# Filling behind the exact chain in priority, gates moved in front, memory's keys and values moved beside the delta rule

## The chip, the cores and the metric

One core of one Trainium2 chip runs the whole program in one launch. The metric is the device time of one execution in microseconds. Times come from repeated runs; the profile is of one execution of its own.

## The reference, cut to what matters

A model of three blocks on 512 tokens of width 1024. The change lies in the mixer of the first block alone:

```
mod = silu(c) @ ada_w + ada_b                      # six vectors of 1024
h = rms(x) * (1 + sc1) + sh1                       # the normed tokens
q_a, kv_a, gate_a, qkv_b, beta_b, a_b, z_b, merge = split(h @ w_in)
y_a = nsa(q_a, kv_a, gate_a)                       # sparse attention, 8 heads, 3 branches
y_b = gated_deltanet(conv(qkv_b), beta_b, a_b, z_b)  # delta rule, 8 heads, chunks of 64
#     decay: g = -exp(a_log) * softplus(a_b + dt_bias), cumulated
#     output: rms(o) * silu(z_b)
y = sigmoid(merge_0) * (y_a @ w_br_a) + sigmoid(merge_1) * (y_b @ w_br_b)
x = x + g1 * (y @ w_out)
```

Two later layers attend to a memory of 256 rows. Its keys and values, `rms(mem) @ x_wkv` for each of the two layers, depend on nothing else, so the kernel may compute them anywhere before.

## The kernel before, in words

A float32 product is done as three products of rounded parts: each operand is split in a high and a low part (`whi`, `wlo`; `ha`, `hl` for the normed tokens), and `mm3` adds high x high, high x low and low x high in PSUM. `gemm_fm` loads a weight block of 128 x 1024 (`wraw`, on SP's queue), splits it on ACT and then on DVE or POOL in turns, and multiplies: 24 products of 512 columns for the tokens, 24 of 256 for memory.

The exact chain (`exact_rstd`, `exact_mod`, `exact_decay`) follows the reference's order of additions to the bit: the norm, 32 paths for the modulation (tiles `xa`, `xd`, `xdc`, `xtc`, `xw`), 64 units for the decay's raw values (`aa`, `ad`, `at` and `adg` of ones and weights, `ahh`), then `decay_sums`, an exact softplus and cumulated sums of small operations. A unit goes PE, ACT, POOL, PE, ACT, then a scan on DVE, in two PSUM banks "x". Its result, the cumulated decay, is what the delta rule starts with.

`front` is the filling: memory's keys and values (`xkv`, two layers), `small1`, the convolutions for the delta rule (`dn_convs`), and sparse attention (`nsa`: compression, head part, body). `among` runs the chain as main and the filling as a generator; each DVE operation of the chain calls `spend`, which adds to a debt and advances the filling until its yields have paid it. So the order of the program interleaves both. A scheduler with a model of times then orders each engine's instructions: at each moment the ready instruction with the lowest priority number goes first, and the number counts up with the order of the program. It also gives tiles their bytes; a tile waits for the tile that had its bytes or its PSUM bank.

After the front the PSUM banks are divided anew and the delta rule runs: `dn_setup`, then `dn` with preparation, heads (two at a time, by turns with the next preparation) and two recurrences. `by_turns` advances `aside` once a round: 16 merge gates (`gates1`), each followed by two steps of `ada`. The output gates `dn_z` stand beside the last heads. Then `merge1` reads the gates back from memory.

Of the kernel before, what the change touches and what calls it, by code (L numbers as in the profile page):

```python
# [267 lines left out]
class Net:  # L268
    def __init__(self, ctx, tc, I, O):
        self.ctx, self.tc, self.nc, self.I, self.O = ctx, tc, tc.nc, I, O  # L270
        nc = self.nc
# [16 lines left out]
        self.gated = self.DR.tile([24, 128, S], F32, name="gated")  # L288
        self.dnd = self.DR.tile([12, 128, S], F32, name="dnd")
        self.mod = self.G.tile([128, 48], F32, name="mod")  # L290
# [41 lines left out]
    def among(self, other, ratio, main):  # L332
        self.other, self.ratio, self.debt = other, ratio, 0.0
        main()
        self.other = None
        for _ in other:
            pass

    def spend(self, out, more=0.0):
        if self.other is not None:  # L340
            self.debt += more or self.ratio * (0.2 + math.prod(out.shape[1:]) / 960)
            other, self.other = self.other, None
            while other is not None and self.debt > 0:
                c = next(other, None)
                if c is None:
                    other = None
                else:
                    self.debt -= c
            self.other = other

# [952 lines left out]
    def gates1(self, T):  # L1303

        for i in range(16):
            p = self.gemm_fm(self.I["w1_fm"][25 + i], self.ha, self.hl)
            self.nc.sync.dma_start(self.gated[i], self.sigmoid(T, p, [128, S], "mg"))
            yield

# [79 lines left out]
    def aside(self, A):  # L1389

        gates, ada = self.gates1(A), self.ada(A)
        for _ in range(16):
            next(gates)
            yield
            for _ in range(2):
                next(ada)
                yield
        for _ in ada:
            pass

    def dn(self, T, W):

        self.dT, self.dW = T, W
        self.pairs = [None] * 4
        turns = self.by_turns
        turns(self.dn_prep(0))
        turns(self.dn_head(0, 0), self.dn_head(0, 1), self.dn_prep(1))
        turns(self.dn_head(1, 0), self.dn_head(1, 1), self.dn_prep(2))
        turns(self.dn_head(2, 0), self.dn_head(2, 1), self.dn_recur(0))
        turns(self.dn_prep(3), self.dn_z(0))  # L1410
        turns(self.dn_head(3, 0), self.dn_head(3, 1), self.dn_gate(0))
        turns(self.dn_recur(1), self.dn_z(1))
        turns(self.dn_gate(1))

    def dn_convs(self, W):

        for pr in range(4):
            for c in (0, 4, 8):
                o = W.tile([128, S], F32, name="draw", bufs=2)
                self.conv_silu(W, o, 9 + c + pr, c + pr)  # L1420
                yield 4
                if c < 8:
                    sq = W.tile([128, S], F32, name="rsq", tag="rsq", bufs=1)
# [5 lines left out]
                self.nc.sync.dma_start(self.dnd[c + pr], o)  # L1429
                yield 2  # L1430

    def dn_prep(self, pr):
# [42 lines left out]
        P.update(qd=qd, kd=kd, kb=kb, kw=kw, vb=vb, at=T.tile([128, 2, 4, 128], F32, name="at", bufs=3),  # L1475
                 wt=T.tile([128, S], F32, name="wt", bufs=3), u=T.tile([128, 4, 128], F32, name="u", bufs=3))
        yield

    def dn_head(self, pr, par):
# [5 lines left out]
        def b4(p):  # L1485
            return p.rearrange("p (b i) -> p b i", b=4)
# [20 lines left out]
        for b in range(4):  # L1507
            c = slice(b * 128, (b + 1) * 128)
            self.mm(p[:, c], k[R, c], q[R, c])
        self.tt(P["at"][:, par], b4(p), mg, OP.mult)  # L1510
        yield
# [47 lines left out]
    def dn_recur(self, hf):  # L1559
# [6 lines left out]
        for c in range(8):  # L1566
# [25 lines left out]
            for hh in range(2):  # L1592
                H = slice(64 * hh, 64 * hh + 64)
                for pp in range(2):
                    self.mm(po[H, pp * 64:pp * 64 + 64], st[H, pp, :], P[pp]["qd"][H, cols])
                    self.mm(px[H, pp * 64:pp * 64 + 64], vn[R, pp, H], P[pp]["at"][R, hh, b, 64 * par:64 * par + 64])
            self.act(o[:, :, cols], po.rearrange("p (a d) -> p a d", a=2))
# [3 lines left out]

    def dn_z(self, hf):

        W = self.dW
        self.zs = []
        for pp in range(2):
            pz = self.gemm_fm(self.I["w1_fm"][21 + 2 * hf + pp], self.ha, self.hl)
            z = W.tile([128, S], F32, name="zg%d" % pp, tag=("kw", "vb")[pp], bufs=2)
            self.act(z, pz)
            s = self.sigmoid(W, z, [128, S], "cs")  # L1610
            self.tt(z, z, s, OP.mult)
            self.zs.append(z)
            yield

    def dn_gate(self, hf):
        W, o = self.dW, self.do
        for pp in range(2):
            self.rms64(W, o[:, pp, :], o[:, pp, :], self.pv("dng"), "do")
            self.tt(self.yb[:, 2 * hf + pp, :], o[:, pp, :], self.zs[pp], OP.mult)
            yield  # L1620
# [43 lines left out]
    def front(self, M):  # L1664

        for l in range(2):
            with self.pool("xf") as T:
                yield from self.xkv(T, l)
        self.small1(M)
        yield 5  # L1670
        with self.pool("dnC") as T:
            yield from self.dn_convs(T)
        with self.pool("nsaT") as T:
            yield from self.nsa(T)

    def block1_mixer(self, ctx):
        pool = self.pool
        with self.weights(2) as self.W, pool("Ya") as A, pool("sm") as M:
            self.ya = A.tile([128, 4, S], F32, name="ya")
            with ExitStack() as B:  # L1680
                with pool("X", side="right") as X:
                    with self.banks({"x": 2, "g": 3, "t": 2, "o": 1}, {"s": "g"}) as self.PS, pool("XR", side="right") as XR:
                        def main():
                            self.exact_rstd(XR)
                            self.fast_mod()
                            self.adaln1()
                            self.ratio = 0.7
                            self.exact(X)
# [400 lines left out]
    def xkv(self, T, l):  # L2089

        nc, I = self.nc, self.I
        m = T.tile([128, KT, 256], F32, name="mem")
        nc.sync.dma_start(m, I["memT"])
        r = self.rstd_x(T, m, 256)
        mh = T.tile([128, KT, 256], F32R, name="memh")
        ml = T.tile([128, KT, 256], F32R, name="meml")
        for k in range(KT):
            g = self.pv("g_mem", 8 * l + k)
            self.act(mh[:, k, :], m[:, k, :], AF.Copy, scale=g)
            self.stt(ml[:, k, :], m[:, k, :], g, mh[:, k, :].bitcast(F32), OP.mult, OP.subtract)  # L2100
        rt = T.tile([128, 2], F32, name="memr")
# [10 lines left out]
        for n in range(4):  # L2112
            pp = self.ps("g")
            for c in range(2):
                hi, lo = self.wslab(I["x_wv%d" % l][n * 2 + c])
                for kk in range(4):
                    k = 4 * c + kk
                    for b in range(2):
                        tk = slice(b * 128, b * 128 + 128)
                        self.mm3(pp[:, b * 256:(b + 1) * 256], mh[:, k, tk], ml[:, k, tk], hi[:, kk, :], lo[:, kk, :],  # L2120
                                 k == 0 and b == 0, k == 7 and b == 1)
            o = T.tile([128, 2, 256], F32, name="mvo", bufs=2)
            for b in range(2):
# [622 lines left out]
```

## Time and profile before

| | us |
|---|---|
| median of 3 runs | 4422.09 (4418.08 to 4423.69) |
| the profiled execution | 4420.88 |
| its span, first to last instruction | 4419.1 |
| PE busy in it | 4036.6 (91%) |
| weight loads (PEld) | 3236.0 (73%) |
| DVE, ACT, POOL busy | 2728.1, 2114.6, 1692.5 |

Busy time of an engine is the time in which at least one of its instructions runs, idle time the rest. PE is TensorE, PEld its weight loads, which overlap its products. The granted clock is TensorE's, as a share of full speed.

### The profile page before, as it was taken

The page shows a single profiled execution, that of the slowest core. Times are in us where ns is not written, and L with a number is a line of the kernel's source. Part 1 is how long each engine was busy: PE and PEld are TensorE (multiplying, and loading weights), DVE is VectorE, ACT ScalarE, POOL GpSimd, SP SyncE. Part 2 cuts the span into 40 slices and gives each one's busy share as a digit, 9 for nine tenths or more (in the row PEclk, how much of TensorE's full clock was granted, in tenths as well). Part 3 has the DMA queues.
Part 4 walks back from the last instruction along what each step waited for, and adds up shares of the span by engine and source line. Part 5 has one row for each costly group of instructions (what it writes and reads, how often), then busy time and mean ns, then how long its engine had stood idle before and what let it go on. Part 6 is the DMA issues. An engine that isn't in the chain of part 4 may idle for free. (4 is left out here: it accounts for less than half of the span.)

```text
span 4419.1 us, 55886 instructions
## 1 busy us (share of the span) xinstructions
PE 4036.6 (91%) x20436; PEld 3236.0 (73%) x20436; DVE 2728.1 (62%) x4770; ACT 2114.6 (48%) x3424; POOL 1692.5 (38%) x1144
## 2 busy tenths in 40 slices
PE   6999799869987989799899999999999899999998
PEld 4887676658866767678676777888777677777886
DVE  6657777677655778576566655332587475665542
ACT  4565668733332768433365544442344365444432
POOL 3342676523222353233254422332344264423431
PEclk8999899979978999899999999999999899999999
DMA  4432210034215889312131332223212122422232
GB/s 154 161 123 70 91 39 8 8 130 146 82 63 186 322 315 376 117 59 70 54 109 66 112 125 71 96 91 98 73 58 75 60 86 79 134 96 81 96 92 80
DMA packets 179605, 480.55 MB, mean 109 GB/s; under 512 B 17576, under 2 KB 28904, under 8 KB 178944
## 3 DMA queue, kind: packets, MB, share of 16 engines
q1 hardware_dynamic: 172512, 452.79, 30.0%
q0 software_dynamic: 6816, 24.15, 1.6%
q8 instruction: 163, 2.67, 0.2%
q14 instruction: 114, 0.93, 0.1%
HBM read 433.31 MB, written 41.44 MB: 107 GB/s over the span
## 5 line engine op out<-in xcount | busy, mean ns | idle before, releaser
L377 POOL TENSOR_TENSOR wlo<-wraw,whi 128x1024 fp32r<-128x1024 f32 (+4 forms) x244 | 554.9, 2274 | 1172.9 <-ACT whi L329 1118.0
L329 ACT ACTIVATE whi<-wraw 128x1024 fp32r<-128x1024 f32 (+4 forms) x489 | 481.7, 986 | 934.6 <-PE ps_g L317 746.6
L317 PE MATMUL ps_g<-ha,whi 128*128 128x512 f32 x2184 | 884.6, 405 | 48.3 <-DVE mraw L357 22.8
L317 PE MATMUL ps_g<-hl,whi 128*128 128x512 f32 x2184 | 887.5, 407 | 0.0
L317 PE MATMUL ps_g<-ha,wlo 128*128 128x512 f32 x2184 | 878.6, 403 | 0.0
L317 PEld LDWEIGHTS ps_g<-ha,whi 128*128 128x128 f32 x2184 | 417.5, 191 | 157.7 <-DVE mraw L357 22.3
L317 PEld LDWEIGHTS ps_g<-ha,wlo 128*128 128x128 f32 x2184 | 417.0, 191 | 100.2 <-issue 5.0
L317 PEld LDWEIGHTS ps_g<-hl,whi 128*128 128x128 f32 x2184 | 417.7, 191 | 97.6 <-issue 5.3
L377 DVE TENSOR_TENSOR wlo<-wraw,whi 128x1024 fp32r<-128x1024 f32 (+4 forms) x245 | 296.1, 1208 | 205.3 <-ACT whi L329 198.6
L353 DVE TENSOR_TENSOR_SCAN aa<-aa 128x774 f32<-128x774 f32 x64 | 126.1, 1971 | 51.1 <-ACT aa L329 46.8
L317 PE MATMUL ps_g<-fah,wlo 128*128 128x512 f32 x352 | 137.0, 389 | 0.0
L317 PE MATMUL ps_g<-fal,whi 128*128 128x512 f32 x352 | 137.0, 389 | 0.0
L317 PE MATMUL ps_g<-fah,whi 128*128 128x512 f32 x352 | 136.9, 389 | 0.0
L367 DVE SCALAR_TENSOR_TENSOR h_R<-h_R,h_gd,ps_s 128x64 f32<-128x64 f32 x448 | 124.7, 278 | 11.9
L329 ACT ACTIVATE aa<-ps_x,aM 128x512 f32<-128x512 f32 x128 | 110.8, 949 | 33.1 <-PE ps_x L317 21.0
L317 PE MATMUL ps_g<-mlo,xh 128*128 128x512 f32 x272 | 111.4, 409 | 14.2 <-POOL mlo L1946 14.2
L2347 POOL TENSOR_SCALAR mP<-mP,sfst 128x512 f32<-128x512 f32 x64 | 102.5, 1609 | 52.6 <-DVE sfst L2346 41.7
L2561 POOL TENSOR_SCALAR g2z<-g2z 128x512 f32<-128x512 f32 x48 | 81.9, 1706 | 95.0 <-DVE g2z L357 82.3
L1517 POOL TENSOR_TENSOR dnl<-dnn,dnc 128x512 f32<-128x512 f32 x48 | 67.1, 1408 | 125.6 <-PE ps_t L317 84.6
L329 ACT ACTIVATE g2z<-g2z 128x512 f32<-128x512 f32 x144 | 90.4, 628 | 49.7 <-POOL g2z L2561 48.1
L329 ACT ACTIVATE mhi<-mrawa 128x2048 fp32r<-128x2048 f32 x52 | 99.6, 1915 | 30.0 <-PE ps_g L317 11.2
L357 DVE TENSOR_TENSOR mlo<-mrawb,mhi 128x2048 fp32r<-128x2048 f32 x42 | 102.8, 2470 | 15.6 <-ACT mhi L329 15.6
(988 smaller groups left out, 10183.8 us busy)
## 6 DMA issues: line engine op xcount, KB each, us to landing
wraw<-w_fm SPq DMA_DIRECT2D x169, 512.0 KB, 3.4
wraw<-f_w SPq DMA_DIRECT2D x120, 512.0 KB, 3.5
mrawa<-moe_g SPq DMA_DIRECT2D x18, 1024.0 KB, 10.6
mrawb<-moe_d SPq DMA_DIRECT2D x18, 1024.0 KB, 8.3
adaw<-ada_w SPq DMA_DIRECT2D x64, 256.0 KB, 3.1
mrawa<-moe_u SPq DMA_DIRECT2D x16, 1024.0 KB, 9.3
mrawb<-moe_u SPq DMA_DIRECT2D x16, 1024.0 KB, 10.5
mrawb<-moe_g SPq DMA_DIRECT2D x14, 1024.0 KB, 10.4
```

Of the source, the lines that this page charges most:

```text
L317: self.nc.tensor.matmul(out, a, b, start=start, stop=stop)
L329: return self.nc.scalar.activation(out, in_, f, **kw)
L353: return self.nc.vector.tensor_tensor_scan(out, *args, **kw)
L357: return self.nc.vector.tensor_tensor(out, a, b, op=op)
L367: return self.nc.vector.scalar_tensor_tensor(out, a, s, b, op0=op0, op1=op1)
L377: e.tensor_tensor(lo, src, hi, op=OP.subtract)
L1517: nc.gpsimd.tensor_tensor(nl, n_, dnc[:, 1 + lv, None, :].to_broadcast([128, 4, 128]), op=OP.mult)
L2347: nc.gpsimd.tensor_scalar(P, P, st[:, 3:4], None, op0=OP.mult)
L2561: self.nc.gpsimd.tensor_scalar(z, z, ZMIN, None, op0=OP.max)
```

## The change

The filling gets priority numbers of its own, 100000 behind the chain's; it is advanced for the same debt, but only where the debt is positive. The fast modulation and the first norm run ahead of the filling. `xkv` leaves `front`; it works on the bytes of `ha` and `hl`, which the delta rule no longer reads, and replaces the merge gates in `aside`. The merge gates and the four output gates go behind the convolutions in `front`; the output gates are stored in `dnd` and loaded again in `dn_gate`. The tile `at` keeps only the two 64 x 64 squares on its diagonal, which frees bytes.

```
     def among(self, other, ratio, main):
         self.other, self.ratio, self.debt = other, ratio, 0.0
+        self.behind = self.tc.cur_priority + 100000
         main()
         self.other = None
+        self.tc.cur_priority = self.behind
...
     def spend(self, out, more=0.0):
         if self.other is not None:
             self.debt += more or self.ratio * (0.2 + math.prod(out.shape[1:]) / 960)
+            if self.debt <= 0:
+                return
             other, self.other = self.other, None
+            ahead, self.tc.cur_priority = self.tc.cur_priority, self.behind
...
+            self.behind, self.tc.cur_priority = self.tc.cur_priority, ahead
             self.other = other
...
     def gates1(self, T):
...
-            yield
+            yield 5.5
...
     def aside(self, A):
-        gates, ada = self.gates1(A), self.ada(A)
-        for _ in range(16):
-            next(gates)
-            yield
-            for _ in range(2):
-                next(ada)
+        ada = self.ada(A)
+        for l in range(2):
+            for i, _ in enumerate(self.xkv(A, l)):
                 yield
+                for _ in range(1 + (i % 3 == 2)):
+                    next(ada)
+                    yield
...
-        turns(self.dn_prep(3), self.dn_z(0))
+        turns(self.dn_prep(3))
...
-        turns(self.dn_recur(1), self.dn_z(1))
+        turns(self.dn_recur(1))
...
     def dn_convs(self, W):
...
+        for i in range(4):
+            z = W.tile([128, S], F32, name="draw", bufs=2)
+            self.act(z, self.gemm_fm(self.I["w1_fm"][21 + i], self.ha, self.hl))
+            s = self.sigmoid(W, z, [128, S], "cs")
+            self.tt(z, z, s, OP.mult)
+            self.nc.sync.dma_start(self.dnd[12 + i], z)
+            yield 6
...
-        self.tt(P["at"][:, par], b4(p), mg, OP.mult)
+        for i in range(2):
+            H, c = slice(64 * i, 64 * i + 64), slice(64 * i, 64 * i + 64)
+            self.tt(P["at"][H, par], b4(p)[H, :, c], mg[H, :, c], OP.mult)
...
     def dn_gate(self, hf):
...
+            z = W.tile([128, S], F32, name="zg%d" % pp, tag=("kw", "vb")[pp], bufs=2)
+            self.nc.sync.dma_start(z, self.dnd[12 + 2 * hf + pp])
...
     def front(self, M):
-        for l in range(2):
-            with self.pool("xf") as T:
-                yield from self.xkv(T, l)
         self.small1(M)
         yield 5
         with self.pool("dnC") as T:
             yield from self.dn_convs(T)
+            yield from self.gates1(T)
...
-                        fill = self.front(M)
-                        next(fill)
-                        self.among(fill, 0.3, main)
+                        self.exact_rstd(XR)
+                        self.fast_mod()
+                        self.adaln1()
+                        self.among(self.front(M), 0.7, lambda: self.exact(X))
...
     def xkv(self, T, l):
-        m = T.tile([128, KT, 256], F32, name="mem")
-        nc.sync.dma_start(m, I["memT"])
-        r = self.rstd_x(T, m, 256)
-        mh = T.tile([128, KT, 256], F32R, name="memh")
-        ml = T.tile([128, KT, 256], F32R, name="meml")
+        mh, ml = (t[:, 4 * l:4 * l + 4, :].rearrange("p a (b n) -> p (a b) n", b=2) for t in (self.ha, self.hl))
+        acc = T.tile([128, 256], F32, name="ssacc")
         for k in range(KT):
+            m = T.tile([128, 256], F32, name="mem", bufs=2)
+            nc.sync.dma_start(m, I["memT"][:, k, :])
+            sq = acc if k == 0 else T.tile([128, 256], F32, name="sssq")
+            self.act(sq, m, AF.Square)
+            if k:
+                self.tt(acc, acc, sq, OP.add)
```

## Rows read from the trace of the kernel before

**Rows 1.** The page's head.

```profile
span 4419.1 us, 55886 instructions
```

**Rows 2.** Stretches: length, each engine's busy time (instructions), granted clock, DMA share, GB/s.

```profile
core 0: us, PE busy (x) PEld busy (x) DVE busy (x) ACT busy (x) POOL busy (x), PEclk, DMA share, GB/s
0.00:66.00 66.00, 25.63 (x132) 23.07 (x132) 58.75 (x220) 28.04 (x65) 22.26 (x17) 0.84 0.42 149
...
0.00:171.00 171.00, 124.22 (x736) 95.31 (x736) 104.17 (x266) 72.19 (x140) 51.31 (x40) 0.93 0.46 157
171.00:937.00 766.00, 672.03 (x3558) 526.64 (x3556) 549.93 (x984) 495.00 (x879) 386.34 (x370) 0.92 0.20 66
...
500.00:850.00 350.00, 325.22 (x1676) 245.50 (x1675) 243.98 (x337) 253.00 (x432) 239.63 (x240) 0.96 0.08 27
870.00:937.00 67.00, 34.27 (x110) 20.60 (x108) 58.57 (x294) 28.70 (x84) 7.14 (x23) 0.61 0.22 75
937.00:990.00 53.00, 46.45 (x204) 36.88 (x205) 35.98 (x58) 16.40 (x30) 16.32 (x12) 0.84 0.47 159
990.00:1256.00 266.00, 254.52 (x1871) 222.56 (x1870) 183.85 (x328) 88.34 (x144) 85.38 (x56) 0.98 0.30 100
```

**Rows 3.** Stretches, only instructions on memory's high part: PE, PEld, DVE, ACT, clock.

```profile
0.00:66.00 66.00, 16.79 (x64) 13.41 (x64) 5.13 (x8) 3.29 (x8) 0.84 0.42 149
...
171.00:280.00 109.00, 59.47 (x304) 49.43 (x304) 4.38 (x8) 3.30 (x8) 0.98 0.49 161
sum 280.00, PE 104.78 PEld 85.63 DVE 9.52 ACT 6.59; mean PE 26.20 PEld 21.41 DVE 2.38 ACT 1.65
```

**Rows 4.** The delta-rule stage, only instructions on the normed tokens' high part.

```profile
937.00:1300.00 363.00, 115.73 (x320) 62.78 (x320) 0.00 (x0) 0.00 (x0) 0.91 0.30 100
```

**Rows 5.** PE in order of time, a path's identity product: start, length, instruction.

```profile
76.14 1.02 PE L317 MATMUL ps_x<-xd,cst 128*128 128x512 f32 x2
...
81.32 1.07 PE L317 MATMUL ps_x<-xd,cst 128*128 128x512 f32 x2
```

**Rows 6.** Stretches, only instructions on the chain's PSUM tiles: PE, PEld, DVE, ACT.

```profile
490.00:660.00 170.00, 96.05 (x443) 70.32 (x443) 2.56 (x4) 66.70 (x78) 0.94 0.15 51
660.00:870.00 210.00, 134.88 (x637) 94.81 (x636) 0.00 (x0) 96.18 (x112) 0.97 0.03 8
```

**Rows 7.** POOL's and DVE's groups, 500 to 860: busy, mean ns | idle before.

```profile
L1006 POOL TENSOR_TENSOR ad<-aa 128x512 f32<-128x512 f32 x61 | 86.7, 1422 | 19.0 <-ACT aa L329 18.6 <-ACT vcp L329 0.4
L973 POOL TENSOR_TENSOR at<-tri,awp 128x512 fp32r<-128x512 f32 (+1 forms) x56 | 66.5, 1216 | 13.4 <-PE ps_x L317 13.4
L973 POOL TENSOR_TENSOR adg<-cst,awp 128x256 fp32r<-128x256 f32 x56 | 55.6, 1024 | 6.3 <-PE ps_x L317 6.2
...
L353 DVE TENSOR_TENSOR_SCAN aa<-aa 128x774 f32<-128x774 f32 x61 | 120.7, 1981 | 51.0 <-ACT aa L329 46.8 <-POOL ad L1006 1.8 <-ACT pth L329 1.2
```

**Rows 8.** POOL and DVE in order of time, 31 to 39.

```profile
31.13 2.00 POOL L867 TENSOR_TENSOR xsq<-xtk 128x1024 f32<-128x1024 f32 x1 [1.22 <-issue]
31.20 1.95 DVE L367 SCALAR_TENSOR_TENSOR xprc<-xeyc,xerc 128x8 f32<-128x8 f32 x1
...
38.50 0.16 DVE L367 SCALAR_TENSOR_TENSOR xprc<-xeyc,xerc 128x8 f32<-128x8 f32 x1
```

**Rows 9.** Stretch 171 to 937, NSA's body: queries, probabilities, values, compressed values.

```profile
171.00:937.00 766.00, 47.16 (x128) 25.28 (x128) 8.99 (x8) 4.98 (x8) 0.92 0.20 66
...
171.00:937.00 766.00, 32.41 (x160) 21.15 (x160) 35.35 (x72) 70.90 (x200) 0.92 0.20 66
...
171.00:937.00 766.00, 42.60 (x128) 24.30 (x128) 1.26 (x2) 1.09 (x2) 0.92 0.20 66
...
171.00:937.00 766.00, 5.44 (x16) 2.51 (x16) 4.29 (x5) 1.22 (x4) 0.92 0.20 66
```

**Rows 10.** DVE in order of time, the ends of the last two heads before the last.

```profile
875.86 0.68 DVE L357 TENSOR_TENSOR ya<-ps_o,P 64x512 f32<-64x512 f32 x1 [0.17 <-ACT P L329]
...
897.05 0.68 DVE L357 TENSOR_TENSOR ya<-ps_o,P 64x512 f32<-64x512 f32 x1
```

**Rows 11.** DMA issues of the page: KB each, median us to landing.

```profile
wraw<-w_fm SPq DMA_DIRECT2D x169, 512.0 KB, 3.4
```

More of the change, by code (lines that the diff above doesn't have):

```diff
@@ L288, in __init__ @@
         self.gated = self.DR.tile([24, 128, S], F32, name="gated")
-        self.dnd = self.DR.tile([12, 128, S], F32, name="dnd")
+        self.dnd = self.DR.tile([16, 128, S], F32, name="dnd")
         self.mod = self.G.tile([128, 48], F32, name="mod")
@@ L1474, in dn_prep @@
         self.tt(v4(vb), pvv.rearrange("p (b h d) -> p b h d", b=4, h=2), bc(self.smt[:, :, 32:40]), OP.mult)
-        P.update(qd=qd, kd=kd, kb=kb, kw=kw, vb=vb, at=T.tile([128, 2, 4, 128], F32, name="at", bufs=3),
+        P.update(qd=qd, kd=kd, kb=kb, kw=kw, vb=vb, at=T.tile([128, 2, 4, 64], F32, name="at", bufs=3),
                  wt=T.tile([128, S], F32, name="wt", bufs=3), u=T.tile([128, 4, 128], F32, name="u", bufs=3))
@@ L1595, in dn_recur @@
                     self.mm(po[H, pp * 64:pp * 64 + 64], st[H, pp, :], P[pp]["qd"][H, cols])
-                    self.mm(px[H, pp * 64:pp * 64 + 64], vn[R, pp, H], P[pp]["at"][R, hh, b, 64 * par:64 * par + 64])
+                    self.mm(px[H, pp * 64:pp * 64 + 64], vn[R, pp, H], P[pp]["at"][R, hh, b])
             self.act(o[:, :, cols], po.rearrange("p (a d) -> p a d", a=2))
@@ L1600, in dn_recur @@
             yield
[L1602 to L1613, printed above, removed]
     def dn_gate(self, hf):
@@ L1617, in dn_gate @@
         for pp in range(2):
+            z = W.tile([128, S], F32, name="zg%d" % pp, tag=("kw", "vb")[pp], bufs=2)
+            self.nc.sync.dma_start(z, self.dnd[12 + 2 * hf + pp])
             self.rms64(W, o[:, pp, :], o[:, pp, :], self.pv("dng"), "do")
-            self.tt(self.yb[:, 2 * hf + pp, :], o[:, pp, :], self.zs[pp], OP.mult)
+            self.tt(self.yb[:, 2 * hf + pp, :], o[:, pp, :], z, OP.mult)
             yield
@@ L1682, in block1_mixer @@
                     with self.banks({"x": 2, "g": 3, "t": 2, "o": 1}, {"s": "g"}) as self.PS, pool("XR", side="right") as XR:
[L1683 to L1688, printed above, removed]
-                        fill = self.front(M)
-                        next(fill)
-                        self.among(fill, 0.3, main)
+                        self.exact_rstd(XR)
+                        self.fast_mod()
+                        self.adaln1()
+                        self.among(self.front(M), 0.7, lambda: self.exact(X))
                     Yb = B.enter_context(pool("Yb"))
@@ L2091, in xkv @@
         nc, I = self.nc, self.I
-        m = T.tile([128, KT, 256], F32, name="mem")
-        nc.sync.dma_start(m, I["memT"])
-        r = self.rstd_x(T, m, 256)
-        mh = T.tile([128, KT, 256], F32R, name="memh")
-        ml = T.tile([128, KT, 256], F32R, name="meml")
-        for k in range(KT):
-            g = self.pv("g_mem", 8 * l + k)
-            self.act(mh[:, k, :], m[:, k, :], AF.Copy, scale=g)
-            self.stt(ml[:, k, :], m[:, k, :], g, mh[:, k, :].bitcast(F32), OP.mult, OP.subtract)
+        mh, ml = (t[:, 4 * l:4 * l + 4, :].rearrange("p a (b n) -> p (a b) n", b=2) for t in (self.ha, self.hl))
+        acc = T.tile([128, 256], F32, name="ssacc")
+        for k in range(KT):
+            m = T.tile([128, 256], F32, name="mem", bufs=2)
[4 more added lines that the diff above has]
+                self.tt(acc, acc, sq, OP.add)
+            g = self.pv("g_mem", 8 * l + k)
+            self.act(mh[:, k, :], m, AF.Copy, scale=g)
+            self.stt(ml[:, k, :], m, g, mh[:, k, :].bitcast(F32), OP.mult, OP.subtract)
+        p = self.ps("t")
+        self.mm(p[:, :256], self.ones, acc)
+        r = T.tile([128, 256], F32, name="memn")
+        self.rsqrt(self.dW, p[:, :256], D, 256, r)
         rt = T.tile([128, 2], F32, name="memr")
@@ L2121, in xkv @@
                                  k == 0 and b == 0, k == 7 and b == 1)
-            o = T.tile([128, 2, 256], F32, name="mvo", bufs=2)
+            o = T.tile([128, 2, 256], F32, name="mvo")
             for b in range(2):
```

## The prediction

> **What bounds the kernel now.** I read the page first, then stage windows, then single tiles. The profiled execution took 4420.88 us for a span of 4419.1 us [rows 1]; everything the change touches lies before 1296 us, so all sums below are about that stretch, and the 1.8 us around the span stay. I took TensorE as the clock of the account: wherever work is to be moved, I ask what becomes of PE's busy time and of its idle time.
>
> The stage windows [rows 2] show a front from 0 to 937 us (exact chain with filling) and a delta-rule stage from 937 to 1296 us. To 171 us, the stretch in which the normed tokens are made, PE is busy 124.2 us, idle 46.8; from there to 937 busy 672.0 of 766, idle 94.0. So the front holds 140.8 us of idle PE. In its middle (500 to 850) PE is busy 325 of 350 us, 7% idle; at its end (870 to 937) the softplus and cumulative sums run as small operations on DVE (58.6 of 67 us) and PE is busy half the time at a mean granted clock of 0.61. The delta-rule stage between 990 and 1256 is bound by PE: 254.5 of 266 us, with every other engine far below.
>
> **What moves, on PE.** Memory's keys and values leave the front: 104.8 us of PE, nearly all before 280 us [rows 3]. The sixteen merge gates and four output gates come in: their 20 products now take 115.7 us in the delta-rule stage [rows 4], 5.8 us each. The front gains 10.9 us of PE work. In the other direction the delta rule gives 115.7 and takes xkv. At full clock 304 of the 512 products that read its high part took 59.5 us [rows 3], so all take 59.5 x 512 / 304 = 100.2: the stage loses 15.5 us of PE work.
>
> Small parts I cost at nothing. The halved `at` replaces one DVE product of 128 partitions by two of half the size, eight times, under a DVE that is busy 184 of 266 us while PE sets the pace [rows 2]; a DVE operation on 64 partitions x 512 takes 0.68 us [rows 10], so uncovered it is 5 us at most. The four output gates now go out to memory and come back. Their loads need a buffer that an earlier pair's `kw` or `vb` held and `dn_gate` follows a recurrence that they hide under; behind them on SP stand only the loads for the merge. Uncovered, each costs less than the 3.4 us of a weight block twice its size [rows 11], once per half. The loads of memory are cut in eight, 16 issues on SP for 2 before; the weight blocks change places (32 for 20 in the delta-rule stage). In the front each merge gate's store stands on SP behind three ACT operations that now give way to the chain, and the next weight blocks stand behind the store; two blocks are loaded ahead, and what that cover lacks is in the idle shares below.
>
> **The front, stage by stage.** Filling now has a number 100000 behind the chain, so the chain goes first wherever it is ready.
>
> Start: before 66 us PE is busy 25.6 us [rows 2], 16.8 of which is xkv [rows 3]. Without it 8.8 us of work is left, so if nothing moves up PE idles 57 us. DVE was busy 58.8 of 66 us there, and xkv's low parts alone held it for 5.1 (its squares' sums, weight parts and evacuations come on top), so the exact norm and the activated condition should be ready some 9 us sooner: 57 - 8.8 = 48 us idle. Bounds 40 and 57.
>
> The modulation's 32 paths: where the chain ran without filling, the identity product of one path started 5.2 us after that of the path before, with PE continuously busy [rows 5]. The chain fills PE by itself: 32 x 5.2 = 166 us, little room for filling and little idle, 8 us (0 to 15).
>
> The decay's 64 units: the chain's own PE time is 96.1 + 134.9 = 231 us for nearly all of them [rows 6], 3.7 us each, 237 in all. On POOL and DVE the same units cost more: 86.7 + 66.5 + 55.6 on POOL and 120.7 on DVE for 61 of them [rows 7], 329.5 / 61 = 5.4 us if these do not overlap. They do hold each other up: while POOL squares 1024 columns for 2.0 us, a DVE operation on 8 columns takes 1.95 us instead of 0.16 [rows 8]. [...] By overlap instead of turns a unit would be bounded by POOL's 3.4 us, below PE's 3.7, and this stage would leave no room for filling. I take 64 x 5.4 = 346 us, in which 109 us of PE are for the filling. With no filling all of it idles; at the 7% of the middle now, 24 us. The same engines and nearly the same filling make the second the nearer row, strict priority makes it worse: 10%, 35 us.
>
> The rest of gates and NSA's head: all PE work of the front is 796.3 + 10.9 = 807 us. Take off 166 and some 29 for the fast modulation, 237 and the 74 filled in beside the units, and NSA's body, and 174 us remain, mostly products that need little else: 6% idle, 11 us (5 to 20).
>
> NSA's body then runs with no chain beside it. Its PE time is 47.2 + 32.4 + 42.6 + 5.4 = 127.6 us [rows 9]. A head without the chain took 897.05 - 875.86 = 21.2 us [rows 10], so eight take 170 and PE idles 42. If part of it still runs beside the chain, 7% or 9 us.
>
> Idle of the new front: 48 + 8 + 35 + 11 + 42 = 144 us, against 140.8: +3. PE work: +10.9. The end of the chain no longer stands alone: the 34.3 us of PE work at clock 0.61 [rows 2] would be 21 at full clock, -13. The front comes out 1 us longer. What the hidden end of the chain gives, the lone NSA takes back.
>
> **Delta rule.** -15.5 us of PE where PE sets the pace. Its opening (937 to 990) has 6.5 us of idle at clock 0.84 [rows 2]; its constants no longer wait for the chain and load under NSA's last head: -6. The second recurrence keeps its length, its steps follow each other. Bounds for the whole stage: -32 (the opening shrinks to its 39 us at full clock) to 0, where 12 more weight blocks and the norms cost DVE what PE saves. I take -20, one part rounded down for xkv's preparation.
>
> **Sum:** +1 - 20 = -19; 4420.9 - 19 = 4402 for an execution like the profiled one; the median shown is 1.2 us above that execution, so I predict 4403. About 0.2% (9 us) is what a measurement of this kernel can tell from no change.
>
> **Rivals.** First, the filling really fills. The decay idles 24 us, part of NSA's body falls beside the chain (25 idle instead of 42) and the gates cost 6: -33 more, 4369. For it: the program's middle did as well with filling ordered by hand [rows 2]. Against: the convolutions come first in the filling, and they use DVE as the chain does.
>
> Second, nothing to be measured: the delta rule's saving is lost to DVE and the front stays as it is, 4415 to 4425. For it: PE's total is the same up to 5 us, and the chain was held by its own POOL and DVE turns [rows 7], which a priority does not shorten.
>
> Third, slower: the filling is starved in the decay. The convolutions' products need DVE operations with two SBUF inputs to give their PSUM banks back; if the chain's turns with POOL leave these late, three "g" banks stand full and PE takes only half of its 109 us: 72 idle instead of 35, +37, 4439. It decides against the change from 29 us more idle in that stage on. [...] The row of the middle, 7% idle under the same turns, speaks against.
>
> **Chances and range.** The forecast 0.38 (own range 4388 to 4412), the full filling 0.22, no change 0.17, the starved filling 0.23. Faster by over 9 us are 0.32 of the forecast's 0.38, the whole of the full filling and 0.04 of no change, together 0.58; slower are 0.23 and 0.01 of no change, 0.24; 0.18 is left for the same. The range runs past the full filling by half its worth, 4354, and takes in most of the starved one, 4442.
>
> **What would show it.** Right: xkv's products after 900 us, idle PE before them near 48 us at the start; units of the decay at 5 to 5.8 us; the chain's small operations over well before NSA ends; a head of NSA alone near 21 us; the stretch of the delta rule about 15 us shorter. Wrong: units of the decay at 6 us or more with PE under 85% there (slower); heads of NSA near 16 us each with the chain gone (faster); a delta-rule stage in which DVE, not PE, ends the waits.

## The result, and the profile after

The changed kernel takes 4464.2 us (median of 4 runs, 4461.54 to 4465.24) where the kernel before took 4421.43 in runs beside it: a ratio of 1.0096, 95% interval 1.0083 to 1.0109. It is 43 us slower; the prediction was 18 us faster, with a range that ended at 4442.

The page's head of the kernel after:

```profile
span 4463.0 us, 56009 instructions
```

Stretches of the kernel before, then of the kernel after, cut where the last work ahead of the delta rule ends and where its output is complete (columns as in [rows 2]):

```profile
0.00:938.00 938.00, 796.96 (x4293) 622.62 (x4294) 654.41 (x1250) 567.55 (x1021) 437.76 (x410) 0.92 0.24 82
938.00:1296.00 358.00, 324.33 (x2335) 275.87 (x2333) 235.93 (x448) 116.73 (x197) 101.58 (x68) 0.91 0.29 98
```

```profile
0.00:970.00 970.00, 840.29 (x3992) 634.32 (x3992) 635.99 (x1201) 581.31 (x1031) 425.52 (x403) 0.90 0.22 72
970.00:1341.00 371.00, 311.04 (x2635) 286.90 (x2635) 259.83 (x504) 107.64 (x187) 118.26 (x74) 0.87 0.38 126
```

Both stages are longer: the front by 32 us, the delta rule by 13, together 45 of the span's 43.9; what follows is 1 us shorter. The two have different reasons. In the front PE idles less (970 - 840.3 = 129.7 us for 141.0) but is busy 43.3 us more, of which the moved products, by the prediction's rows, explain 10.9. In the delta rule PE does 13.3 us less, as wanted, and idles 60.0 us for 33.7.

The front of the kernel after, stretch by stretch: start, modulation, the chain's constants before the decay, 64 units, the chain's small operations, the rest:

```profile
0.00:58.00 58.00, 12.54 (x57) 10.50 (x57) 48.18 (x198) 19.76 (x44) 19.83 (x17) 1.00 0.33 115
58.00:348.00 290.00, 268.51 (x1411) 208.26 (x1412) 175.97 (x160) 164.46 (x289) 99.38 (x74) 0.95 0.27 89
348.00:408.00 60.00, 55.58 (x228) 42.63 (x227) 57.35 (x144) 37.57 (x61) 26.94 (x31) 0.97 0.36 121
408.00:835.00 427.00, 398.17 (x1999) 307.93 (x1998) 264.94 (x301) 285.95 (x442) 272.85 (x273) 0.96 0.17 57
835.00:907.00 72.00, 58.75 (x161) 35.45 (x161) 64.07 (x312) 39.10 (x108) 0.00 (x0) 0.55 0.04 12
907.00:967.00 60.00, 46.45 (x139) 29.38 (x139) 23.45 (x79) 33.53 (x90) 6.51 (x9) 0.56 0.21 71
```

The last two lines matter most. After 835 no weight block is left: sparse attention's body runs first beside the chain's small operations on DVE (busy 64 of 72 us), then alone, and PE, busy 80% of the time but stopping and starting, is granted 0.55 of its clock for 132 us. Before, the low stretch at the front's end was 67 us long with 34 us of PE in it [rows 2].

What that does to the body is seen on its own instructions. Kernel after, the same four tiles as in [rows 9] (queries, probabilities, values, compressed values):

```profile
0.00:1000.00 1000.00, 59.78 (x128) 31.40 (x128) 6.54 (x8) 4.99 (x8) 0.89 0.23 75
0.00:1000.00 1000.00, 43.35 (x160) 25.44 (x160) 35.88 (x72) 70.00 (x200) 0.89 0.23 75
0.00:1000.00 1000.00, 53.12 (x128) 30.10 (x128) 1.26 (x2) 1.09 (x2) 0.89 0.23 75
0.00:1000.00 1000.00, 7.45 (x16) 3.06 (x16) 4.08 (x5) 1.23 (x4) 0.89 0.23 75
```

The counts are the same 128, 160, 128 and 16; PE's time on them is 163.7 us for 127.6, 36 us more for the same work. The first line alone, beside the units and after them:

```profile
744.00:835.00 91.00, 19.59 (x54) 10.66 (x54) 4.49 (x5) 3.12 (x5) 0.94 0.03 10
835.00:967.00 132.00, 40.18 (x74) 20.74 (x74) 2.06 (x3) 1.87 (x3) 0.55 0.12 38
```

A product of the queries takes 0.36 us in the first stretch and 0.54 in the second; its four widths stand in nearly equal shares in both. The ends of the last four heads (DVE in order of time) are 23.2, 20.7 and 19.8 us apart, about the 21.2 us of [rows 10]:

```profile
903.39 0.68 DVE L363 TENSOR_TENSOR ya<-ps_o,P 64x512 f32<-64x512 f32 x1 [0.28 <-ACT P L329]
926.55 0.69 DVE L363 TENSOR_TENSOR ya<-ps_o,P 64x512 f32<-64x512 f32 x1 [1.28 <-ACT P L329]
947.27 0.68 DVE L363 TENSOR_TENSOR ya<-ps_o,P 64x512 f32<-64x512 f32 x1 [0.48 <-ACT P L329]
967.06 0.68 DVE L363 TENSOR_TENSOR ya<-ps_o,P 64x512 f32<-64x512 f32 x1
```

The delta rule's stage of the kernel after, what PE waited for (us in total, times, longest):

```profile
PE ps_t L317 <- DVE memn L416: 7.3, 2, 4.3
PE ps_g L317 <- ACT ha L329: 7.2, 4, 3.0
PE ps_t L317 <- DMA gchl<-rlo: 6.9, 1, 6.9
PE ps_g L317 <- DVE mvo L368: 6.6, 1, 6.6
...
PE ps_t L317 <- DVE gin L1369: 3.1, 1, 3.1
```

None of these five is in the same view of the kernel before, where the gates, ready at once, filled PE while the constants came in. The places of the first three, PE in order of time:

```profile
980.19 0.98 PE L317 MATMUL ps_t<-gchl,dns 128*128 128x8 f32 x4 [6.89 <-DMA gchl<-rlo]
...
986.33 0.58 PE L317 MATMUL ps_g<-ha,whi 128*128 128x256 f32 x1 [1.47 <-ACT ha L329]
...
995.57 0.58 PE L317 MATMUL ps_g<-ha,whi 128*128 128x256 f32 x1 [3.03 <-ACT ha L329]
...
1002.79 1.08 PE L317 MATMUL ps_t<-cst,memn 1*128 1x64 f32 x4 [4.35 <-DVE memn L416]
```

Memory's first products go a few at a time, as fast as its parts are split; then all of PE's queue stands behind the norm. The stage's opening:

```profile
970.00:1022.00 52.00, 30.09 (x159) 25.17 (x160) 37.45 (x75) 20.78 (x51) 11.42 (x9) 0.64 0.52 166
```

### The profile page after: what moved, and what is told of

It is laid out like the page before. It is cut to its first block, busy times and chain, and to the rows that moved or that the text cites. A ratio compares the mean times of both kernels' runs of the same rounds, so it can differ in the third digit from the quotient of the medians.

```text
span 4463.0 us, 56009 instructions
## 1 busy us (share of the span) xinstructions
PE 4064.8 (91%) x20436; PEld 3255.8 (73%) x20436; DVE 2736.4 (61%) x4778; ACT 2120.1 (48%) x3424; POOL 1696.4 (38%) x1144
## 5 line engine op out<-in xcount | busy, mean ns | idle before, releaser
L317 PE MATMUL ps_g<-ha,whi 128*128 128x512 f32 (+1 forms) x2312 | 921.1, 398 | 53.2 <-DVE mraw L363 22.6
L317 PE MATMUL ps_g<-hl,whi 128*128 128x512 f32 (+1 forms) x2312 | 923.1, 399 | 0.3 <-DVE hl L373 0.3
L317 PE MATMUL ps_g<-ha,wlo 128*128 128x512 f32 (+1 forms) x2312 | 916.1, 396 | 0.8 <-DVE wlo L383 0.8
L317 PEld LDWEIGHTS ps_g<-ha,whi 128*128 128x128 f32 x2312 | 443.0, 192 | 164.5 <-DVE mraw L363 22.2
L317 PEld LDWEIGHTS ps_g<-ha,wlo 128*128 128x128 f32 x2312 | 442.2, 191 | 102.0 <-issue 5.2
L317 PEld LDWEIGHTS ps_g<-hl,whi 128*128 128x128 f32 x2312 | 443.1, 192 | 100.2 <-issue 5.5
L329 ACT ACTIVATE mhi<-mrawb 128x2048 fp32r<-128x2048 f32 x50 | 95.7, 1915 | 35.6 <-PE ps_g L317 23.7
L317 PE MATMUL ps_g<-mhi,xh 128*128 128x512 f32 x272 | 109.9, 407 | 2.0 <-ACT xh L329 2.0
```

The costliest lines, as they stand in the source:

```text
L317: self.nc.tensor.matmul(out, a, b, start=start, stop=stop)
L329: return self.nc.scalar.activation(out, in_, f, **kw)
```

## The experiments

Fourteen kernels. "Front" is the time at which the last work ahead of the delta rule ends (the chain, sparse attention, or filling behind it), "stage" from there to the delta rule's complete output, "body" PE's time on the four tiles above. These three come from one profiled execution of each kernel, which can lie off the median: 4468.7 us in e6, 4427.3 in e11, 4439.1 in e14. The kernels are read for their times alone; that e8 to e12 compute the reference's result is not claimed.

| run | us | ratio to before (95%) | front | stage | body |
|---|---|---|---|---|---|
| before | 4421 | 1 | 938 | 358 | 127.6 |
| after | 4464.2 | 1.0096 (1.0083 to 1.0109) | 970 | 371 | 163.7 |
| e1_moves_only | 4442.1 | 1.0047 (1.0030 to 1.0063) | 948 | 370 | 143.9 |
| e2_priority_only | 4472.8 | 1.0116 (1.0099 to 1.0133) | 991 | 360 | 169.2 |
| e3_x_bank | 4460.7 | 1.0092 (1.0076 to 1.0109) | 967 | 371 | 162.2 |
| e4_gates_in_nsa | 4470.0 | 1.0111 (1.0094 to 1.0127) | 975 | 369 | 160.7 |
| e5_nsa_first | 4449.8 | 1.0060 (1.0044 to 1.0077) | 940 | 388 | 116.6 |
| e6_nsa_first_plain | 4456.4 | 1.0073 (1.0056 to 1.0090) | 972 | 370 | 131.5 |
| e7_gates_open | 4465.6 | 1.0099 (1.0083 to 1.0116) | 938 | 402 | 157.1 |
| e8_gates_last | 4459.1 | 1.0076 (1.0059 to 1.0093) | 972 | 365 | 135.6 |
| e9_norm_early | 4449.9 | 1.0060 (1.0043 to 1.0077) | 968 | 358 | 162.9 |
| e10_prep_early | 4466.6 | 1.0101 (1.0084 to 1.0118) | 983 | 355 | 160.9 |
| e11_plain_spread | 4432.8 | 1.0020 (1.0011 to 1.0030) | 936 | 365 | 130.7 |
| e12_mem_in_body | 4441.4 | 1.0045 (1.0028 to 1.0062) | 998 | 322 | 137.6 |
| e13_plain_mem | 4448.4 | 1.0058 (1.0043 to 1.0074) | 991 | 328 | 132.5 |
| e14_plain_both | 4433.9 | 1.0024 (1.0015 to 1.0033) | 987 | 324 | 118.1 |

**The two halves apart.** e1 takes out the priority:

```
-        self.behind = self.tc.cur_priority + 100000
...
-            ahead, self.tc.cur_priority = self.tc.cur_priority, self.behind
...
-            self.behind, self.tc.cur_priority = self.tc.cur_priority, ahead
```

> The changed kernel with the filling's priority numbers taken away: it is advanced for the same debt, but takes its numbers in program order as before; all moved work stays moved. Theory A (two costs: the front's, +32 us, comes from the priority, which lets the gates run early beside the chain and leaves sparse attention's last 135 us without other products at a granted clock of 0.55; the delta rule's, +13 us, comes from the move of the gates): the front ends near 940 again, the delta-rule stage still takes about 370 us, 4430 to 4436 us. Theory B (the whole loss comes from what was moved, the priority changes little): the front still ends near 970, 4458 to 4466. [...]

e2 adds only these lines (and the end of `among`) to the kernel before.

> The kernel before with the one edit that the filling's numbers stand 100000 behind the chain's; nothing is moved. Theory A: the delta-rule stage keeps its 358 us, the front is longer by 15 to 30 us with a stretch of sparse attention alone at its end at a clock under 0.65: 4436 to 4452. Theory B: within 0.2% of before, 4412 to 4430. My prediction's own working (chain ahead shortens the front where nothing is moved): under 4412.

Front and stage of e1, then front of e2:

```profile
0.00:948.00 948.00, 824.81 (x3992) 623.91 (x3992) 638.86 (x1201) 575.64 (x1030) 422.02 (x403) 0.92 0.22 74
948.00:1318.00 370.00, 309.66 (x2635) 284.81 (x2635) 260.23 (x504) 107.98 (x187) 118.13 (x74) 0.87 0.38 126
```

```profile
0.00:991.00 991.00, 841.21 (x4295) 650.96 (x4296) 678.52 (x1248) 569.08 (x1021) 445.65 (x410) 0.88 0.24 78
```

The stage is 370 us with the moves and 360 without them: its 12 or 13 us belong to the moves. The priority lengthens the front by 22 us on top of the moves and by 53 on its own, where my prediction's working had it shorter. e1 and e2 were some 6 and 20 us over their expected times. The front of the moves alone is 10 us longer; that this is near the 10.9 us of PE work predicted for it is chance. A front is PE's busy time plus its idle time, so it can be put together from three terms, each against before: the body's PE time, the moved work at its predicted 10.9, PE's idle time. After: +36 +11 -11 = +36, measured +32. e1: +16 +11 -18 = +9, measured +10. e2: +42 +0 +9 = +51, measured +53. What is left over is 4 us at most. The account does not say by itself that the body's slow products set the length: where they take less of it, idle time can stand in their place, as in e6 and e8 below.

**The chain's end.** e3 gives it a bank of its own.

```
     def decay_sums(self, T, a, na):
-        pt = self.ps("t")
+        pt = self.ps("x")
```

> The changed kernel with one PSUM bank changed: the end of the chain (decay_sums) takes a bank x, which only the chain uses, in place of a bank t, which sparse attention's transposes use. In the changed kernel this end stands at 907 us until 966, when sparse attention is done. Theory A (the chain's product waits for its bank, which sparse attention's earlier allocations hold, whatever its priority): the transposed decay is out before 915 us, the delta rule's opening (970 to 1020, PE busy 28 us) shortens by 5 to 12 us, 4451 to 4459. Rival (the order on PE or the tiles' bytes hold it, not the bank): it stays at 966, 4460 to 4467.

The transposed decay on ACT, in the kernel after and in e3:

```profile
965.96 0.27 ACT L329 ACTIVATE agr<-ps_t 32x128 f32<-32x128 f32 x1 [0.58 <-PE ps_t L326]
```

```profile
911.01 0.27 ACT L329 ACTIVATE agr<-ps_x 32x128 f32<-32x128 f32 x1
```

The wait for the bank is shown: first in priority, the chain stood 55 us behind a bank that the filling held. The time is not won, 4460.7: the first loads for the delta rule's constants start at 966 to 967, when sparse attention is done, as in the kernel after, and the opening keeps its wait of 7.1 us for the constants' DMA. That these loads wait for sparse attention's bytes follows from the program and fits e8 below. The expected 5 to 12 us did not come.

**The order of the filling.** e4 advances one gate per five units of the body's yields; e5, and e6 without priority, put sparse attention first; e8 puts the gates behind it:

```
         with self.pool("dnC") as T:
             yield from self.dn_convs(T)
-            yield from self.gates1(T)
         with self.pool("nsaT") as T:
             yield from self.nsa(T)
+        with self.pool("gat") as T:
+            yield from self.gates1(T)
```

> The changed kernel with the 16 merge gates spread over sparse attention's body (one per about six of its units of yield) in place of standing right behind the convolutions. Theory A (the lone body runs at half clock for want of other products): the body starts some 90 us earlier beside the chain, the front's last 135 us show a granted clock over 0.8 in place of 0.55, and the front ends 20 to 40 us earlier: 4422 to 4445. Theory C (POOL's and DVE's turns set the units, products are no matter): units stay at 6.5 us, the front keeps its length: 4458 to 4468.

> The changed kernel with the order of the filling turned: sparse attention first, then the convolutions, output gates and merge gates. Theory A (the front is long because what the strict priority leaves to its end is sparse attention's body, a series of short dependent steps on which PE stops and goes at a granted clock of 0.55): the end of the front now holds dense products, its last 100 us show a clock over 0.85, the front ends 25 to 55 us earlier (915 to 945), 4408 to 4440. Theory C (the chain's units on POOL and DVE set the front, whatever fills): the units stay over 6.3 us, the front ends within 10 us of 970: 4454 to 4474.

> The same turned order, with the filling's numbers in program order again (as in the run of the moves alone, 4442 us with a front of 948 us). Theory A: the body runs beside the chain in both, so the order matters less, but the end gains the same way: front 915 to 940, 4408 to 4434. Theory C: front within 10 us of 948, 4432 to 4452. If this one is clearly below the run with priority, the priority itself costs, apart from what it leaves to the end.

> The changed kernel with only the 16 merge gates' place in the filling changed: behind sparse attention in place of ahead of it. Theory A, as the runs so far leave it (strict priority leaves whatever has the last numbers to the end; if that is sparse attention it runs alone at half clock, if it is dense products they run at full clock; in the run with sparse attention first the convolutions were left to the chain's end and DVE, busy 49 of 50 us, bound them): with gates last the end needs neither DVE nor dependent steps: the last 60 us of the front at a clock over 0.9, the front ends at 915 to 940, 4410 to 4436. Theory C (POOL's and DVE's turns): front within 10 us of 970, 4454 to 4474. Theory E (the order on PE is fixed by a model of times that takes gates whenever sparse attention is late, so their place in the order is no matter, as where they were spread over its body): front 960 to 975, 4454 to 4470.

e4 failed to spread anything: the gates were taken as soon as PE was free, the first head ended at 793 as in the kernel after, and the end stayed alone. Its two stretches:

```profile
600.00:800.00 200.00, 197.23 (x944) 153.09 (x942) 103.23 (x110) 136.14 (x202) 129.45 (x127) 0.99 0.20 65
840.00:975.00 135.00, 103.47 (x293) 64.20 (x292) 90.66 (x400) 71.08 (x194) 7.34 (x24) 0.55 0.14 44
```

e5 did what theory A asked: gates alone at the end, at a clock of 0.99, the chain's last product out at 836 in place of 966, the front 30 us shorter, within its expected 915 to 945. The kernel won only 14 us. In the front, the convolutions now met the chain's small operations and DVE was the bound there (first line):

```profile
735.00:850.00 115.00, 77.20 (x270) 56.46 (x271) 103.94 (x323) 63.00 (x110) 16.37 (x29) 0.81 0.28 96
850.00:940.00 90.00, 85.68 (x368) 68.58 (x366) 23.25 (x26) 46.51 (x64) 19.20 (x8) 0.99 0.44 143
```

Of the front's 30 us, 17 were lost again in the stage, 388 us for 371. The loads of its constants begin only when the last gate is done, and PE waits for them:

```profile
PE ps_t L317 <- DMA gchl<-rlo: 15.4, 1, 15.4
PE ps_t L317 <- DMA dnc<-dn_c: 10.4, 1, 10.4
```

e8 came out in the ranges of theories C and E (4459), but not for E's reason: the gates ran at a clock of 0.90 at the end, but none ran beside the chain; from 350 to 450 PE was busy 76.5 of 100 us with DVE at 89.6. In e6, without priority, it was the chain that came last and ran alone, PE busy 24 of the last 72 us. Whatever comes last, the front of these four is 940 to 975 us long. In e6 and e8 PE's time on the body is back to 131.5 and 135.6 us, and the front is 972 all the same, with PE idle for 156 and 144 us in place of 129.7: the low clock on the body is the form that the loss takes in the kernel after, and not its only form.

**The delta rule's stage.** e7 leaves four gates at its start, ahead of memory's products; e9 works memory's norm out once, in the front; e10 splits memory's parts there too, between sparse attention's head part and body:

```
     def aside(self, A):
         ada = self.ada(A)
+        for _ in self.gates1(A, range(12, 16), "mvo"):
+            yield
```

```
     def xkv(self, T, l):
-            self.act(sq, m, AF.Square)
...
-        self.rsqrt(self.dW, p[:, :256], D, 256, r)
+        r, rt = self.memn, self.memr
```

> The changed kernel with four of the 16 merge gates left in the delta-rule stage, ahead of memory's keys and values there. Theory D (the delta-rule stage lost 26 us of PE idle because its opening now holds memory's products, which wait for splits on ACT and DVE and a norm, where before it held gates that were ready at once): the opening's 50 us show over 42 us of PE busy in place of 28, the stage, which gets 23 us more of PE work, grows by less than 12 us from 371, the front loses 23 us of PE work: 4440 to 4456. Rival (the stage is bound by the evictions out of its single bank for products, 24 products in place of 16 and 4): the stage grows by the whole 23 us, idle over 55 us as now, 4458 to 4468.

> The changed kernel with memory's norm worked out once, behind the output gates in the front, in place of twice in the delta-rule stage; the split of memory's parts stays there. Theory D2 (the stage's additional idle of PE is memory's preparation, twice: products that start and stop with the splits, then a wait for the norm; not the absence of gates): the waits for the norm, 7.3 us, go, and some of the stop and go with fewer operations on ACT and DVE: the stage shortens by 6 to 14 us from 371; 4450 to 4459. Rival (evictions out of the single bank): 4460 to 4468.

> As the run before, and the split of memory's parts for both layers is moved as well, to the front behind the last product on the normed tokens, beside sparse attention's body. Nothing of memory's preparation is left in the delta-rule stage. Theory D2: the stage shortens by 16 to 26 us from 371, its opening holds over 40 us of PE busy in 50, 4438 to 4450. Rival (evictions): the stage keeps at least 362 us, 4455 to 4466.

Stage of e7, e9 and e10:

```profile
938.00:1340.00 402.00, 336.99 (x2731) 307.06 (x2731) 271.71 (x510) 119.24 (x204) 121.43 (x76) 0.87 0.38 124
```

```profile
968.00:1326.00 358.00, 306.94 (x2623) 285.17 (x2623) 255.04 (x487) 100.26 (x162) 117.42 (x74) 0.88 0.39 124
```

```profile
983.00:1338.00 355.00, 304.62 (x2623) 283.94 (x2623) 252.57 (x471) 92.99 (x148) 116.87 (x74) 0.89 0.37 120
```

Theory D fell with e7: ready gates at the start only push memory's first splits, products and norm 23 to 31 us back, the stage grows by all of their work and more (402), idle 65 us. The rival there, evictions out of the single bank, had the time right (4465.6); but in e9, with that bank unchanged, the stage's wait for the norm goes. D2 holds in e9: the stage is 13 us shorter, 9 of them idle, and so is the kernel (14 us). e10 takes 3 us more off the stage and loses 15 in the front, where the splits now stand ahead of the body. Of the 26 us of additional idle, then, some 9 to 10 are memory's preparation; the constants' DMA (6 to 7 us) and one eviction of memory's values (6.6 us in e9 too) are still there, and the rest is not accounted for. Two buffers for these values (in e11) left that last wait at 6.6 us; what holds it was not settled.

**Filling the body.** e11 is e1 with the gates spread over the body in program order, and with e9's norm; e12 is e10 with memory's first layer's products in the body's second half; e13 is e12 without priority, e14 adds the gates in the first half.

```
+            for c in self.nsa_body(A, kn, qn, vhl, vc, pth, ptl):
+                yield c
+                n += c
+                if n > 0:
...
+                    n -= 3.0
+                    yield next(mem, 0.01)
```

> The moves alone, without the priority (4442 us; front 948 us, delta-rule stage 370 us, PE 144 us on sparse attention's body), with three edits: the 16 merge gates spread over the body, memory's norm worked out once in the front, and two buffers again for memory's values. Theory A with D2: norm and buffer take 13 to 18 us from the stage as they did in the changed kernel; the gates, in program order now really beside the body, keep the clock up, PE's time on the body falls under 132 us and the front ends at 925 to 945: 4405 to 4430. Rival (as with priority, spreading changes nothing): front 945 to 960, 4424 to 4438.

> The run with memory's preparation in the front (4466.6 us; front 983 us, stage 354 us), and besides the 12 groups of products for memory's first layer are moved from the delta-rule stage into the second half of sparse attention's body. Theory A (the end of the front is long because PE starts and stops there at half clock): PE's time on the body falls from about 164 us to under 145, the granted clock of the front's last 100 us is over 0.7, the front grows by less than 30 us for some 50 us of products, the stage shortens by 40 to 50: 4436 to 4457. Rival (dependent steps on ACT and DVE set the end, the clock only shows it): the products add their whole time, front 1025 to 1040, and what the stage saves is lost: 4460 to 4476.

> The last run (memory's preparation and first layer beside sparse attention's body) with the filling's numbers in program order again. Theory A (what fills the front's end decides, the priority only says what is left for it): base is the run of the moves alone, 4442 us; the norm gives 13 us of the stage, the first layer's products another 40 for 15 to 25 us of front: 4400 to 4424. Rival (the priority costs by itself, whatever fills the end, 22 us as between the changed kernel and the moves alone): 4412 to 4424 too, but with the front 20 us shorter than with priority and the body's PE time the same 137 us. Rival 2 (neither: the end is full, products add their whole time): 4434 to 4450.

> The run before with the 16 merge gates also beside sparse attention's body, in its first half (memory's first layer stays in the second). Theory A: both halves of the body then have dense products beside them; PE's time on the body under 128 us, mean granted clock of the front over 0.94, 4392 to 4418, at the lower end faster than the kernel before. Rival 2: the front gets longer by what the stage saves, 4425 to 4445.

The front's last 100 us in e10 and e12:

```profile
883.00:983.00 100.00, 75.79 (x238) 47.68 (x237) 56.00 (x230) 52.94 (x143) 6.52 (x9) 0.62 0.17 55
```

```profile
898.00:998.00 100.00, 88.27 (x468) 69.17 (x469) 57.95 (x199) 52.17 (x125) 18.44 (x14) 0.79 0.37 120
```

This is the nearest test of the clock, and not a clean one, since the splits of memory's parts also moved, from ahead of the body into its middle. Twelve groups of products more (8 x 24 and 4 x 48 instructions of 256 columns, an estimated 50 us at full clock, half of the prediction's 100.2), and the front grows by 15 us: PE's time on the body falls from 160.9 to 137.6 at a clock that rises from 0.62 to 0.79 in these 100 us, and PE idles 18 us less in the front. The last six heads themselves took 165 us for 135; the other 15 us came back ahead of them, where the splits had stood. The stage shortens by 33 us (40 to 50 expected), the kernel by 25.

In e11, with gates really beside the body, its PE time is 130.7 and the front 936 us, both as expected; the time, 4432.8, is in the rival's range, because the stage fell to 365 us only, 5 us under e1's where 13 to 18 were expected. e13 says that the priority costs nothing beyond what it leaves for the end: with the same work beside the body the kernel without priority is 7 us slower than e12, not faster. The time lies in rival 2's range, not in theory A's: the end had less room left (body 143.9 in e1), and the same products and splits cost 43 us of front. e14 takes the body down to 118.1 us, under that of the kernel before, and comes out at 4433.9, in its rival's range: the gates and memory now crowd the front to 987 us.

Nothing run here beats the kernel before; e11 and e14 come nearest and cannot be told apart. They also show what is left when the body's products no longer run slowly: front and stage together hold 1112 and 1113 us of PE work, 9 and 8 less than before, and 14 and 23 us more of PE's idle time, more than all of it in the stage (54.7 and 61.3 us idle for 33.7).

## Why the prediction was wrong

**The step that failed: "the 34.3 us of PE work at clock 0.61 would be 21 at full clock, -13".** I let the low clock vanish with the chain's lonely end and did not give it to the lone body that took its place. I even had the row: a head alone took 21.2 us in a stretch granted 0.61 [rows 2, 10], and it took about that again. (That row was a head beside the chain's small operations; such heads now took 23 to 24 us, those alone 20 to 21.) But I charged its PE work at the 127.6 us of [rows 9], mostly measured beside the chain, and called the rest idle. Measured, PE's idle time from 835 to 967 is 26.8 us and the body's PE time 36 us more: 163.7 + 26.8 = 190.5 us where I had 127.6 + 42 = 169.6. The -13 then took time off the same body once more, though eight heads at 21.2 us were already priced by a row at the low clock. In the sum of the front -13 had to be about +32; idle was 14 us better than my 144. The pieces of the body are parted by waits for ACT (14.6 + 2.3 us from 835 to 967) and DVE (3.2 + 2.5 + 2.3 + 1.0); the granted clock was 0.55 there with PE 80% busy in pieces, and 0.79 in the front's last 100 us of e12, with dense products between them.

**"The stage loses 15.5 us of PE work": right in size, 13.3, and not a gain.** This step cost as much as the first: the stage came out 13 us longer for my -20, outside my bounds of -32 to 0, the front 32 longer for my +1. My -20 took PE as the bound of the whole stage and -6 for the opening. The opening became the place of the loss: 53 us with 46.5 of PE before [rows 2]; in the 52 us from 970 PE was busy 30.1. I had rounded one part down for memory's preparation; it costs 13 us (e9). And I had written that the constants would be ready under the last head. They were not. The chain's end stood behind a PSUM bank, but that was not what held them: with the chain's end out at 911 (e3) or 836 (e5) PE still waited 7.1 and 15.4 us for them, since their loads began only when the front's last work was done. In e8, where sparse attention is over at 873, the loads were issued from 872 to 904, that wait is gone and the stage is 6 us shorter (365). One rival had the stage's saving lost to DVE; none had PE waiting for what was moved in.

**"The chain goes first wherever it is ready".** It did not keep its own pace. A path of the modulation took 9.1 us (290 / 32) where I had 5.2, a unit 6.7 (427 / 64) where I had 5.4. The reason was no shortage: from 408 to 835 PE was busy 398 of 427 us. A lower number did not always put the chain first. This square of a unit was done on POOL at 612.26, and its product began on PE at 617.11, behind 21 products of a gate in a row (POOL's line, then two of PE's):

```profile
610.85 1.41 POOL L1012 TENSOR_TENSOR ad<-aa 128x512 f32<-128x512 f32 x1
...
612.22 0.40 PE L317 MATMUL ps_g<-ha,wlo 128*128 128x512 f32 x1
...
617.11 1.02 PE L317 MATMUL ps_x<-ad,cst 128*128 128x512 f32 x2
```

Whether a bank or the scheduler's model of times held it there is open. My condition for the slower rival, units of 6 us with PE under 85%, was half met and the rival was wrong: filling was not starved in the decay. That a unit's operations on POOL and DVE never overlap, on which its price of 5.4 us rested, no run shows: [rows 8] are one DVE operation as long as the POOL square beside it. In these 427 us POOL was busy 272.9 and DVE 264.9, the filling's operations among them, together 111 more than the stretch, and a unit took 6.7. Nor are turns of the two seen to set this pace: PE waited 12.0 us for POOL's squares in these 427, and in the first 125 of them, beside gates, it was busy 124.2. No run here varies them.

**Right:** idle PE at the start, 45.5 us to 58 for 48; no full filling; the moved work (+10.9 predicted; without the body, PE's time in the front grew by 7.2 us, in e1 by 11.6); a head alone near 21 us; chain and body no longer end together, but for the chain's last product.

## What to carry to other kernels

A strict priority decides what comes last, and what comes last runs alone: give the end dense, independent products, and keep the pieces with dependent steps beside other work (gates at the end ran at a granted clock of 0.99 in e5 and 0.90 in e8, the body without other products at 0.55 in the kernel after). When work is moved beside a stage bound by PE, count its preparation and what has to be ready when the stage opens, not its products alone. Charge PE's work at the clock of the stretch where it will run; a busy share that seems to rise may be the same work at a lower clock (a product of the queries took 0.36 us at 0.94 and 0.54 at 0.55).

## What was not expected of the hardware

With PE busy 105 of 132 us in short pieces, the granted clock was 0.55 over the whole stretch; with PE busy 30.2 of 35 us just before, beside the chain's units, it was 0.93:

```profile
800.00:835.00 35.00, 30.21 (x144) 21.38 (x145) 22.58 (x45) 26.62 (x54) 8.82 (x25) 0.93 0.03 9
835.00:967.00 132.00, 105.20 (x300) 64.83 (x300) 87.52 (x391) 72.63 (x197) 6.51 (x9) 0.55 0.12 38
```

At the low clock the busy share itself is inflated: by the products of the queries, 0.36 us before 835 and 0.54 after, the 105 us hold work that would take about 70 beside the units (an estimate, 105 x 0.36 / 0.54).

What in these pieces goes with the low clock is open. A third of PE's time from 835 to 967 is transposes, with 14.6 us of waits for ACT before them, and no run tells the transposes from the pauses:

```profile
L326 PE MATMUL ps_t<-cst,P 128*128 128x128 f32 x119 | 35.5, 423 | 14.6 <-ACT P L329 14.6
```

A low busy share alone does not go with it in these rows: the first 58 us stand at 1.00 with PE busy 12.5 of them.
